# Strassen products for four pairs of gate and up rows in a fused decoder trunk, with other placement of TensorE's operands

## The chip, the cores and the metric

The kernel runs as one program on one core of a Trainium2 chip. The core has TensorE (PE, matrix multiply), VectorE (DVE), ScalarE (ACT), GpSimd (POOL) and SyncE (SP); the last only issues DMAs here. ACT and POOL issue DMAs too. Each engine works through its own queue of instructions in order and waits for the others by semaphores. The metric is the device time of one execution in microseconds (us), given as the median of several runs.

## The reference

Two decoder layers over 512 tokens of width 1024, in float32. Layer 0 mixes tokens by causal pooling, layer 1 by differential attention; each is followed by a SwiGLU feed-forward block (FFN) of width 2816.

```python
def reference(x, pool_w, pool_scale, w_qkv, w_o, lam_p, subln_g, rel_table, w_gate,
              w_up, w_down, ln_mix_g, ln_mix_b, ln_ffn_g, ln_ffn_b):
    for i in range(DEPTH):                      # DEPTH = 2
        j = i // N_MIXERS
        if i % N_MIXERS == 0:
            h = _multiscale_pool(x, pool_w[j], pool_scale[j])
        else:
            lambda_init = 0.8 - 0.6 * math.exp(-0.3 * i)
            h = _diff_attention(x, w_qkv[j], w_o[j], lam_p[j], subln_g[j], rel_table, lambda_init)
        x = _layernorm(ALPHA * x + h, ln_mix_g[i], ln_mix_b[i])
        x = _layernorm(ALPHA * x + _swiglu(x, w_gate[i], w_up[i], w_down[i]), ln_ffn_g[i], ln_ffn_b[i])
    return x

def _swiglu(x, w_gate, w_up, w_down):
    return (jax.nn.silu(x @ w_gate) * (x @ w_up)) @ w_down
```

## The kernel before

**Precision.** TensorE multiplies in a reduced float32 format (F32R). Each operand is therefore kept as two tiles: a high part, which ACT makes by a cast (line 89), and a low part, the difference, which DVE makes by a subtraction (line 90). A product is three matmuls: high by high, high by low, low by high (`mm3`, lines 106 to 110). `split` makes both parts of a tile.

**Order.** The kernel is written under a manual schedule: on each engine, and on each DMA queue, instructions run in the order in which the Python code emits them. Buffers rotate within a tag; a new tile waits until the old one in its place is no longer used.

**Weights.** All weights lie in one array `wall` in DRAM, in pieces ("chunks") of 128 by 1024. SP loads a chunk into one of 4 buffers `raw`; `split` makes the pair `wh`, `wl`, of which there are 6 buffers each (`WBUFS`). `ready(n)` emits loads and splits up to chunk n. A gate or up product of 128 hidden columns uses one chunk.

**The FFN, gate and up.** The hidden width is 22 rows of 128 columns (`FB`), kept transposed in `hid` (128 partitions, 22 rows, 512 tokens). Row f of the loop is `order[f]`: rows come in pairs k and k + 11. For each row `product` makes gate and up, each 8 blocks of 128 input channels by three matmuls, 512 tokens wide; the input is `xt`, the layer's normed and transposed input in two halves of 256 tokens with high and low parts. `gated` takes silu on ACT and the multiplication on DVE. The first `early` rows (3 in layer 0, 2 in layer 1) are done in two passes of 256 tokens, since the last two blocks of tokens are still being normed and transposed (`late`).

**The FFN, down.** The product of `hid` and the down weights is done with seven block products instead of eight (a Strassen scheme over halves of the hidden rows, tokens and output columns), named P1, Q5, P6, Q3, P7, P2, Q4 (`DOWN`). It needs sums of blocks of `hid` and sums of blocks of weights:

- `sum_weights` (line 474), 11 times per layer during gate and up: SP loads four 256 KB blocks into tiles b0 to b3, DVE adds four times (line 484), POOL writes four results to DRAM, `tsum` (line 486).
- `sum_hidden` (line 491), after each pair of rows: ACT and DVE split the first block into `a11` (lines 497, 499), DVE makes the differences in place (498, 500) and the two sums `u` (501, 504), ACT casts them to `v` (505). `settle` one product later makes the low part (508) and POOL writes both to DRAM, `ssum` (509).
- In the down stage `prepare` splits weight items a few items ahead, and `left` prepares the left operand of an item in a part of `xt` (P1 uses `a11` as it is; P7 and Q3 are loaded from `ssum` by POOL, line 566). `multiply` does 12 matmuls, 512 wide, for an item of two hidden rows (line 629).

**Other parts that the change touches.** `affine` applies a norm's gain and bias to the residual `res`, two DVE instructions of 1024 (lines 189, 190); the gain and bias come by `load_gb` into a tile of tag `gb`. Attention keeps its transposed heads in tiles `oh`, `ol` (lines 892 to 897), queries and keys in `qh`, `ql`, `kh`, `kl`; `gather` multiplies the heads with the output weights (products `wo`). `turn` transposes a block of `res` on TensorE (line 198). Tiles lie in SBUF in the order of allocation: `res` first (16 KB per partition), then small ones, `xt` (32 KB), `raw` (4 x 4 KB), `wh` and `wl` (12 x 4 KB), the rest of `keep`, and above it the pool of the current stage; in an FFN `hid` (44 KB), then `a11` (22 KB), `u`, `v` and b0 to b3.

## Time and profile before

| | |
|---|---|
| median of 3 runs | 982.99 us (979.09 to 983.11) |
| the profiled execution | 983.17 us, span of its instructions 981.1 us |
| mean granted TensorE clock | 0.995 |
| matmuls | 4974 |

In the profile's pages "PE" is TensorE's matmuls and "PEld" its weight loads, which overlap them. A row of a group names line, engine, operation, output and input tiles, shapes and count; after the first bar stand the busy time and the mean duration of one in ns, after the second the idle time of the engine before these instructions and what ended it. A matmul's duration overlaps with that of its neighbours. DMA rows give the size of one transfer and the median time from issue to landing. A row of stretches gives, for each engine, busy time and number of instructions, then TensorE's clock, the share of DMA engines' time and GB/s.

### The profile page before, as it was taken

To read this page: it belongs to the slowest core of one execution; us is meant where nothing else is said; L and a number is where in the kernel's file an instruction comes from. 1 tells how busy PE (TensorE), PEld (TensorE's weight loads), DVE (VectorE), ACT (ScalarE), POOL (GpSimd) and SP (SyncE) were. 2 spreads that over 40 slices of the span, in tenths; PEclk is the share of its full clock that TensorE was granted. 3 is DMA by queue.
4 is the path that set the end of the run, shared out by engine and by line. 5 is a ranking of instruction groups with operands and counts; after the bars stand their busy time and mean duration, and the time that the engine had idled before them with its cause. 6 is when DMAs were issued, how large, how long until landed. Compare 5 with 4: busy or idle time off the path is not lost.

```text
span 981.1 us, 13416 instructions
## 1 busy us (share of the span) xinstructions
PE 963.2 (98%) x4974; PEld 820.6 (84%) x4974; DVE 643.4 (66%) x1007; ACT 420.5 (43%) x708; POOL 123.7 (13%) x195
## 2 busy tenths in 40 slices
PE   8999999999999999999999999999999999999995
PEld 8898888888888888988888888988888888888884
DVE  6845874455567577688777676756655555477687
ACT  5753222223326357656556554732223322244460
POOL 4201111111120211000000000011111111111102
PEclk9999999999999999999999999999999999999997
DMA  8247768655776984323222122276665566878942
GB/s 223 66 158 247 250 228 289 229 193 193 266 257 236 329 295 151 114 82 94 73 87 86 55 86 86 90 270 211 225 256 193 209 229 228 288 246 297 341 145 86
DMA packets 70079, 188.59 MB, mean 192 GB/s; under 512 B 15956, under 2 KB 16084, under 8 KB 70014
## 3 DMA queue, kind: packets, MB, share of 16 engines
q1 hardware_dynamic: 56588, 141.57, 42.1%
q0 software_dynamic: 13408, 46.15, 13.9%
q8 instruction: 39, 0.64, 0.3%
q14 instruction: 26, 0.21, 0.1%
q10 hardware_dynamic: 18, 0.02, 0.0%
HBM read 150.99 MB, written 36.72 MB: 191 GB/s over the span
## 4 chain that ended last, share of the span: by engine, by line
PE 94%; DVE 3%; ACT 1%; POOL 1%; issue 0%; POOLq 0%; DVEq 0%
PE P L629 13%; PE g L109 8%; PE u L108 8%; PE u L109 8%; PE g L108 8%; PE u L110 8%; PE g L110 8%; PE Q L629 6%; PE s L814 2%; PE v L108 2%; PE v L110 2%; PE v L109 2%; PE wo L108 2%; PE wo L109 2%; PE wo L110 2%; PE q L109 1%
## 5 line engine op out<-in xcount | busy, mean ns | idle before, releaser
L90 DVE TENSOR_TENSOR wl<-raw,wh 128x1024 fp32r<-128x1024 f32 x118 | 141.7, 1220 | 33.3 <-ACT wh L89 33.3
L89 ACT CAST wh<-raw 128x1024 fp32r<-128x1024 f32 x120 | 123.5, 1050 | 65.9 <-PE u L109 63.9
L109 PE MATMUL g<-xt,wh 128*128 128x512 f32 (+1 forms) x392 | 144.1, 368 | 0.5 <-DVE xt L90 0.5
L108 PE MATMUL g<-xt,wh 128*128 128x512 f32 (+1 forms) x392 | 144.3, 368 | 0.0
L108 PE MATMUL u<-xt,wh 128*128 128x512 f32 (+1 forms) x392 | 144.1, 368 | 0.0
L110 PE MATMUL u<-xt,wl 128*128 128x512 f32 (+1 forms) x392 | 144.0, 367 | 0.0
L109 PE MATMUL u<-xt,wh 128*128 128x512 f32 (+1 forms) x392 | 144.0, 367 | 0.0
L110 PE MATMUL g<-xt,wl 128*128 128x512 f32 (+1 forms) x392 | 144.0, 367 | 0.0
L460 DVE TENSOR_TENSOR hid<-sg,u 128x512 f32<-128x512 f32 x44 | 30.3, 688 | 154.9 <-PE u L110 154.5
L90 DVE TENSOR_TENSOR dl<-r,dh 128x1024 fp32r<-128x1024 f32 x84 | 94.3, 1132 | 38.8 <-ACT dh L89 38.7
L89 ACT CAST dh<-r 128x1024 fp32r<-128x1024 f32 x84 | 81.5, 979 | 69.6 <-PE P L629 31.7
L629 PE MATMUL P<-dh,xt 128*128 128x512 f32 x352 | 109.4, 390 | 0.0
L109 PEld LDWEIGHTS g<-xt,wh 128*128 128x128 f32 x392 | 73.9, 189 | 12.7 <-DVE xt L90 0.7
L110 PEld LDWEIGHTS u<-xt,wl 128*128 128x128 f32 x392 | 73.9, 189 | 12.3
L108 PEld LDWEIGHTS u<-xt,wh 128*128 128x128 f32 x392 | 73.9, 189 | 12.1
L110 PEld LDWEIGHTS g<-xt,wl 128*128 128x128 f32 x392 | 73.9, 188 | 12.2
L108 PEld LDWEIGHTS g<-xt,wh 128*128 128x128 f32 x392 | 73.9, 188 | 12.2
L109 PEld LDWEIGHTS u<-xt,wh 128*128 128x128 f32 x392 | 73.9, 188 | 12.0
L505 ACT CAST v<-u 128x512 fp32r<-128x512 f32 x22 | 13.7, 621 | 159.4 <-issue 142.5
L629 PEld LDWEIGHTS P<-dh,xt 128*128 128x128 f32 x352 | 66.1, 188 | 13.6
L484 DVE TENSOR_TENSOR b<-b,b 128x512 f32<-128x512 f32 x88 | 60.8, 691 | 18.4 <-DMA b<-in_wall 16.2
L459 ACT ACTIVATE sg<-g 128x512 f32<-128x512 f32 x44 | 26.3, 599 | 103.5 <-PE g L110 102.0
(189 smaller groups left out, 1792.5 us busy)
## 6 DMA issues: line engine op xcount, KB each, us to landing
raw<-in_wall SPq DMA_DIRECT2D x128, 512.0 KB, 4.2
b<-in_wall SPq DMA_DIRECT2D x88, 256.0 KB, 5.6
tsum<-b POOLq DMA_DIRECT2D x88, 256.0 KB, 4.7
r<-tsum SPq DMA_DIRECT2D x40, 512.0 KB, 4.7
r<-in_wall SPq DMA_DIRECT2D x30, 512.0 KB, 5.0
ssum<-v POOLq DMA_DIRECT2D x22, 512.0 KB, 4.0
xt<-ssum POOLq DMA_DIRECT2D x20, 512.0 KB, 6.0
res<-in_x SPq DMA_DIRECT2D x8, 256.0 KB, 6.4
```

The costliest lines, as they stand in the source:

```text
L89: nc.scalar.copy(dst_h, src)
L90: (low or nc.vector).tensor_tensor(dst_l, src, dst_h.bitcast(F32), op=ALU.subtract)
L108: nc.tensor.matmul(acc, ah, bh, start=start, stop=False)
L109: nc.tensor.matmul(acc, ah, bl, start=False, stop=False)
L110: nc.tensor.matmul(acc, al, bh, start=False, stop=stop)
L459: nc.scalar.activation(sg, pg, AF.Silu)
L460: nc.vector.tensor_tensor(hid[:, f, :], sg, pu, op=ALU.mult)
L484: nc.vector.tensor_tensor(z, x, y, op=ALU.add)
L505: nc.scalar.copy(v[:, :, 0, :], u)
L629: nc.tensor.matmul(accs[s], x[:, k, r], y[:, c], start=first and k == 0 and e == 0, stop=last and k == m - 1 and e == 2, skip_group_check= ...
L814: nc.tensor.matmul(accs[c][:, :wide], a[r, qs], b[r, :wide], start=i == 0, stop=i == 2)
```

## The change

It has four parts.

1. **Strassen for gate and up.** For the pairs of rows k = 4, 6, 7 and 9 (`SPLIT`), in both layers, gate and up are computed together by the same seven-product scheme, over halves of tokens, halves of input channels, and gate against up. Each of the seven products (`GATE`) is 2 rows by 4 blocks by 3 matmuls, 256 tokens wide. Gate and up share three PSUM banks A, C and B; results are copied or subtracted out of a bank between products. The left operands are the quarters of `xt` for P1, P2 and Q4, and four sums of quarters for the others, made once per layer by `sums_of_x` in a new tile `xs`. Their right operands are sums of weight chunks, made in place in the `raw` tiles: `steps` is the written-out order of sums, casts and low parts, and `advance` emits it up to a chunk. The host lays out these chunks differently.
2. **Down sums of weights.** `load_terms` has POOL load the four blocks and then add two more loads on top of two of them (`accum_op`); `sum_terms` leaves two additions to DVE. The blocks lie in rows of `hid` that are not yet used, or in the `gb` tile, and are loaded two sums before they are used, at the rows of a list. `affine` and `load_gb` move for it (the next one behind the loop over rows, or into attention).
3. **Gated sums.** `sum_hidden` becomes a generator that `catch_up` advances one step after each product; `ssum` is written by ACT's queue. `a11` goes; P1's left operand is split in the down stage, and P6's difference is made there.
4. **Placement.** `xt`, a tile of 32 KB called `region` and the 12 weight tiles are allocated first. `region` holds in turn the pooled input, `xs` (also the down product's left operands) and attention's heads, queries and keys.

```diff
 HALF = FB // 2
 DOWN = ("P1", "Q5", "P6", "Q3", "P7", "P2", "Q4")
+SPLIT = (4, 6, 7, 9)
+GATE = ("P1", "Q5", "P6", "Q3", "P7", "P2", "Q4")
...
+    xt = keep.tile([P, 2, 2, KB, 256], F32R, name="xt")
+    def region(name):
+        return keep.tile([P, 8192], F32R, tag="region", name=name)
+    pooled = region("pooled").rearrange("p (i k t) -> p i k t", i=2, k=KB)
+    ph, pl = pooled[:, 0], pooled[:, 1]
+    def weight_pair(name):
+        return tuple(
+            keep.tile([P, 1024], F32R, tag=f"w{q}", name=f"{name}{q}", bufs=WBUFS) for q in "hl"
+        )
+    first_pair = weight_pair("pw0")
...
+            for k in range(HALF):
+                j0 = index[k] = len(chunks)
+                c = c0 + 4 * k
+                if k in SPLIT:
+                    chunks += [(c, ()), (c, (c, c + 1)), (c, (c, c + 2)), (c + 2, ())]
+                    chunks += [(c + 1, (c + 1, c + 2)), (c + 3, ()), (c, (c, c + 3))]
+                    step("cast", j0)
+                    for w in (
+                        "low 0, sum 1, cast 1, sum 4, cast 3, cast 4, low 1, sum 2, cast 2, low 3, "
+                        "low 2, sum 6, cast 5, cast 6, low 4, low 5, low 6"
+                    ).split(", "):
+                        steps.append((w[:-2], j0 + int(w[-1])))
+                else:
+                    for i in range(4):
+                        chunks.append((c + i, ()))
+                        step("cast", j0 + i)
+                        step("low", j0 + i)
...
+            def advance(upto, strict=False):
+                upto = min(upto, len(chunks))
+                while not all(j in finished for j in range(upto)):
+                    kind, j = steps.pop(1 if strict and steps[0][1] >= upto else 0)
+                    c, pair = chunks[j]
+                    refill()
+                    t = raws[c]
+                    if kind == "sum":
+                        tt(t, raws[pair[0]], raws[pair[1]], op=ALU.add)
+                    elif kind == "cast":
+                        halves[j] = weight_pair(f"g{layer}_{j}")
+                        nc.scalar.copy(halves[j][0], t)
+                    else:
+                        h, l = halves[j]
+                        tt(l, t, h.bitcast(F32), op=ALU.subtract)
+                        finished.add(j)
+                    for d in set((c,) + pair):
+                        if uses[d] == (kind, j):
+                            raws.pop(d)
+                            held[0] -= 1
...
+            def ahead(upto):
+                advance(upto)
+                if upto > len(chunks):
+                    prepare(upto - len(chunks), upto - len(chunks))
...
+            def sums_of_x():
+                r0, r1, r2, r3 = spare(4), spare(15), spare(6), spare(17)
+                def whole(t, a, b):
+                    tt(t, quarter(a, 0, b).bitcast(F32), quarter(a, 1, b).bitcast(F32), op=ALU.add)
+                def high(m, t):
+                    nc.scalar.copy(xs[:, m, 0], t)
+                def low(m, t):
+                    tt(xs[:, m, 1], t, xs[:, m, 0].bitcast(F32), op=ALU.subtract)
...
+                whole(r2, 0, 0)
+                yield
+                whole(r3, 0, 1)
+                yield
+                whole(r0, 1, 0)
+                whole(r1, 1, 1)
+                yield
+                tt(r1, r0, r1, op=ALU.subtract)
+                high(0, r1)
+                tt(r0, r2, r0, op=ALU.subtract)
+                high(2, r0)
+                yield
+                tt(r2, r1, r2, op=ALU.subtract)
+                high(1, r2)
+                low(0, r1)
+                yield
+                tt(r3, r3, r2, op=ALU.add)
+                high(3, r3)
+                low(2, r0)
+                yield
+                low(1, r2)
+                yield
+                low(3, r3)
+                yield
...
+            def load_terms(k):
+                i, j = k // 2, k % 2
+                c = slice(j * 512, (j + 1) * 512)
+                if k == 1:
+                    t = [hid[:, row, :] for row in (4, 5, 15, 16)]
+                elif k % 2 == 0 and k < HALF - 1:
+                    t = [hid[:, row, :] for row in (9, 10, 20, 21)]
+                else:
+                    rest = keep.tile([P, 4, 512], F32, tag="gb", name=f"b{layer}_{k}")
+                    t = [rest[:, q, :] for q in range(4)]
+                for q, b in enumerate((0, 1, 3, 2)):
+                    nc.gpsimd.dma_start(out=t[q], in_=block(i, b)[:, c])
+                for q, b in ((0, 1), (1, 3)):
+                    nc.gpsimd.dma_start(out=t[q], in_=block(i, b)[:, c], accum_op=ALU.add)
+                terms[k] = t
...
+            def sum_terms(k):
+                i, j = k // 2, k % 2
+                c = slice(j * 512, (j + 1) * 512)
+                t1, t3, b22, b21 = terms.pop(k)
+                tt(b22, t1, b22, op=ALU.add)
+                tt(b21, b22, b21, op=ALU.add)
+                for m, z in enumerate((t1, b22, t3, b21)):
+                    nc.gpsimd.dma_start(out=tsum[m, i, :, c], in_=z)
+            summed_rows = [0]
+            def weight_sums():
+                k = summed_rows[0]
+                summed_rows[0] += 1
+                sum_terms(k)
+                if k + 2 < HALF - 1 and k != 1:
+                    load_terms(k + 2)
+                if k == HALF - 2:
+                    load_terms(HALF - 1)
...
+            def sum_hidden(k):
+                first, second = hid[:, k, :256], hid[:, k, 256:]
+                a12, a22 = hid[:, k + HALF, :256], hid[:, k + HALF, 256:]
+                u = fp.tile([P, 2, 256], F32, tag="u", name=f"u{layer}_{k}", bufs=1)
+                v = fp.tile([P, 2, 2, 256], F32R, tag="v", name=f"v{layer}_{k}", bufs=1)
+                tt(u[:, 0, :], first, second, op=ALU.subtract)
+                tt(second, second, a22, op=ALU.subtract)
+                tt(u[:, 1, :], a12, first, op=ALU.subtract)
+                tt(u[:, 1, :], u[:, 1, :], second, op=ALU.add)
+                nc.scalar.copy(v[:, :, 0, :], u)
+                yield
+                tt(v[:, :, 1, :], u, v[:, :, 0, :].bitcast(F32), op=ALU.subtract)
+                yield
+                nc.scalar.dma_start(out=ssum[:, :, :, k, :], in_=v.bitcast(F32))
+            def catch_up():
+                for g in list(behind):
+                    if next(g, g) is g:
+                        behind.remove(g)
...
-                if p == "P1":
-                    made[j] += (a11[:, 0, r, :], a11[:, 1, r, :])
-                    return
...
+                o = 2 * (j % 2)
+                t = xs[:, j // 2 % 4, :, o : o + m, :]
...
+                    if p == "P6":
+                        tt(src, hid[:, r, 256:], src, op=ALU.subtract)
...
+            load_terms(0)
+            load_terms(1)
+            sums = sums_of_x()
...
+                        advance(2 * f + 6)
+                        gated(order[f], *accs[f])
+                        affine(n - 1, f)
+                        if f < 2:
+                            weight_sums()
+                            next(sums)
+            behind.append(sum_hidden(0))
...
+            def plain(f):
+                k = f // 2
+                j = index[k] + 2 * (f % 2)
                 a = (bank(f"g{layer}_{f}"), bank(f"u{layer}_{f}"))
                 for i in range(2):
-                    product(a[i], c0 + 2 * f + i, 0, S)
-                    if c0 + 2 * f + 5 + i <= c1:
-                        ready(c0 + 2 * f + 5 + i)
+                    product(a[i], j + i, 0, S)
+                    ahead(j + i + 5)
+                    if f >= 3:
+                        next(sums, None)
+                    catch_up()
+                gated(order[f], *a)
+                if f < SB:
+                    affine(n - 1, f)
+                if f in (3, 5, 6, 7, 10, 11, 16, 17, 20):
+                    weight_sums()
+                if f == 3:
+                    load_terms(3)
+                if f % 2:
+                    behind.append(sum_hidden(k))
+            def strassen(k):
+                names = {"P1": "A", "P6": "A", "P7": "A", "Q4": "A", "Q5": "C", "Q3": "C", "P2": "B"}
+                banks = {b: bank(f"{b}{layer}_{k}") for b in "ACB"}
+                lefts = {
+                    "P1": [quarter(0, i, 0) for i in range(2)],
+                    "P2": [quarter(0, i, 1) for i in range(2)],
+                    "Q4": [quarter(1, i, 1) for i in range(2)],
+                }
+                for m, p in enumerate(("Q5", "P6", "P7", "Q3")):
+                    lefts[p] = [xs[:, m, i] for i in range(2)]
+                rows = hid[:, k : k + HALF + 1 : HALF, :]
+                first, second = rows[:, :, :256], rows[:, :, 256:]
...
+                for j, p in enumerate(GATE):
+                    acc = banks[names[p]]
+                    h, l = halves[index[k] + j]
+                    xh, xl = lefts[p]
+                    for f in range(2):
+                        o = acc[:, f * 256 : (f + 1) * 256]
+                        for kk in range(4):
+                            c = slice((4 * f + kk) * P, (4 * f + kk + 1) * P)
+                            for e, (w, x) in enumerate(((h, xh), (h, xl), (l, xh))):
+                                nc.tensor.matmul(
+                                    o, w[:, c], x[:, kk, :],
+                                    start=p in ("P1", "Q5", "P2") and f + kk + e == 0,
+                                    stop=p in ("Q4", "Q3", "P2") and (f, kk, e) == (1, 3, 2),
+                                    skip_group_check=True,
+                                )
+                    acc = both(acc)
+                    if p == "P1":
+                        g0 = tile_of(0)
+                        nc.scalar.copy(both(g0), acc)
+                    elif p == "Q5":
+                        nc.scalar.copy(second, acc)
+                    elif p == "P6":
+                        nc.scalar.copy(first, acc)
+                    elif p == "Q3":
+                        tt(first, acc, first, op=ALU.subtract)
+                    elif p == "P7":
+                        tt(second, second, acc, op=ALU.subtract)
+                    elif p == "P2":
+                        tt(both(g0), acc, both(g0), op=ALU.add)
+                        nc.scalar.activation(g0, g0, AF.Silu)
                     else:
-                        prepare(2 * f + 5 + i - 2 * FB, 0)
-                    if i == 0:
-                        settle()
-                        if f % 2 == 0 or f in (early, FB - 1):
-                            sum_weights(summed_rows[0])
-                            summed_rows[0] += 1
-                gated(order[f], *a)
-                if f % 2:
-                    sum_hidden(f // 2)
-                if 0 < f - early <= SB:
-                    affine(n - 1, f - early - 1)
-                if f - early == SB + 2:
-                    load_gb(n)
-
-            settle()
+                        g1 = tile_of(1)
+                        nc.scalar.activation(both(g1), acc, AF.Silu)
+                    ahead(index[k] + j + 6)
+                    catch_up()
+                    if p == "P2":
+                        tt(first, both(g0), first, op=ALU.mult)
+                    elif p == "Q4":
+                        tt(second, both(g1), second, op=ALU.mult)
+                behind.append(sum_hidden(k))
...
+            whole = region("heads").rearrange("p (h i t) -> p h i t", h=HEADS, i=2)
+            slots = {h: whole[:, h] for h in range(HEADS)}
+            rest = xt[:, 1].rearrange("p i k t -> p (i k t)").rearrange("p (h i t) -> p h i t", h=4, i=2)
+            slots.update({16 + h: rest[:, h - 6] for h in (6, 7)})
...
+                oh, ol = (slots[h if h < 6 else 16 + h][:, i, :] for i in range(2))
...
+                if h == SB + 1:
+                    load_gb(n)
```

In the diff `hid`'s rows given as 9, 10, 20, 21 and 4, 5, 15, 16 are places for blocks of weights before these rows are computed; `...` marks what is left out, among it the removed `sum_weights`, `a11` and `settle`, and `product` and `gated`, which stay as they were but take the weight pair from `halves`.

198 lines of the change are left out of this document (102 added, 96 removed).

## The prediction

> **What bounds the kernel now.** First the page: busy time, granted clock, and the chain that ended last.
>
> ```profile
> PE 963.2 (98%) x4974; PEld 820.6 (84%) x4974; DVE 643.4 (66%) x1007; ACT 420.5 (43%) x708; POOL 123.7 (13%) x195
> ...
> PEclk9999999999999999999999999999999999999997
> ...
> PE 94%; DVE 3%; ACT 1%; POOL 1%; issue 0%; POOLq 0%; DVEq 0%
> ```
>
> TensorE (PE) carries 94% of the chain at full clock. Busy time alone can hide pipelining, so next the stretches by stage: gate and up of layer 0, its down product, gate and up of layer 1.
>
> ```profile
> core 0: us, PE busy (x) PEld busy (x) DVE busy (x) ACT busy (x) POOL busy (x), PEclk, DMA share, GB/s
> 60.00:284.00 224.00, 224.00 (x1058) 188.42 (x1057) 125.72 (x174) 63.44 (x85) 29.25 (x52) 1.00 0.67 230
> 284.00:383.00 99.00, 99.00 (x439) 81.54 (x438) 73.98 (x94) 50.65 (x65) 13.88 (x20) 1.00 0.75 263
> ...
> 638.00:864.00 226.00, 226.00 (x1030) 188.49 (x1029) 126.36 (x175) 63.04 (x85) 29.70 (x53) 1.00 0.67 234
> ```
>
> In these stretches PE never pauses, while VectorE (DVE) works 56% of gate and up, ScalarE (ACT) 28%. So the price of a matmul is its distance from start to start, read in the timeline (first column: start). One product of 24 matmuls, 512 wide, then one of 24, 256 wide (first and last):
>
> ```profile
> 147.93 0.39 PE L108 MATMUL u<-xt,wh 128*128 128x512 f32 x1
> ...
> 153.37 0.39 PE L108 MATMUL g<-xt,wh 128*128 128x512 f32 x1
> ```
>
> ```profile
> 43.77 0.28 PE L108 MATMUL u<-xt,wh 128*128 128x256 f32 x1
> ...
> 46.53 0.28 PE L110 MATMUL u<-xt,wl 128*128 128x256 f32 x1
> ```
>
> (153.37 - 147.93)/24 = 226.7 ns and (46.53 - 43.77)/23 = 120.0 ns. Half the width costs 0.529 of a full one.
>
> **The change, part 1: fewer columns.** A plain pair of rows (k and k+11) is 4 products, 96 matmuls: 96 x 226.7 = 21.76 us. A Strassen pair is 7 products of 24 matmuls 256 wide: 168 x 120.0 = 20.16 us. Eight pairs: -12.8 us. No row shows the new operand xs. Bounds for its matmul: 113.3 ns (half of 226.7) and 126.9 ns (120.0 plus the 6.9 ns of the next paragraph), which over 1344 matmuls is -9.0 or +9.3 us. I take 120.0, because access pattern and place in SBUF equal the quoted row's.
>
> **Part 2: operands at the low end.** Down products P1 (left operand a11) and Q5 (xt) as pieces of the chain, each of 66 matmuls, then the output projection:
>
> ```profile
> 284.10 15.35 PE P L629 x66
> 299.45 14.97 PE Q L629 x66
> ```
>
> ```profile
> 572.00 0.40 PE L108 MATMUL wo<-wh,oh 128*128 128x512 f32 x1
> ...
> 574.57 0.39 PE L110 MATMUL wo<-wh,ol 128*128 128x512 f32 x1
> ```
>
> 232.6 against 226.8 ns, and 2.57/11 = 233.6 ns. Adding up tile sizes in the code's order, xt and the weights lie in the first 113 KB, a11 begins at 169 KB, oh and ol at 179 KB; the far operands cost 6 to 7 ns more. The change brings all of these into the first 112 KB: 132 P1 matmuls x 5.8 = -0.76 us, 192 wo matmuls x 6.9 = -1.3 us. The Trainium skill (SBUF — State Buffer, § SBUF: two separate sides) lets PE wait on no one and names no dependence on the address; by it this part is worth 0 and the forecast 2 us later. The quoted rows differ, so the trace does not agree. Transposes of res, which moves up: 96 of them, at most 6.9 ns each, 0 to +0.7 us, taken as 0.
>
> Sum of PE time: -12.8 - 0.8 - 1.3 = -14.9 us.
>
> **Part 3: what the other engines get.** Groups of DVE and ACT (mean ns of one stands after the busy time), and two wide subtractions in a row:
>
> ```profile
> L90 DVE TENSOR_TENSOR wl<-raw,wh 128x1024 fp32r<-128x1024 f32 x118 | 141.7, 1220 | 33.3 <-ACT wh L89 33.3
> L484 DVE TENSOR_TENSOR b<-b,b 128x512 f32<-128x512 f32 x88 | 60.8, 691 | 18.4 <-DMA b<-in_wall 16.2
> L498 DVE TENSOR_TENSOR hid<-hid 128x256 f32<-128x256 f32 x22 | 9.3, 424 | 0.7
> L89 ACT CAST wh<-raw 128x1024 fp32r<-128x1024 f32 x120 | 123.5, 1050 | 65.9 <-PE u L109 63.9 <-issue 1.3 <-ACT line L422 0.7
> L459 ACT ACTIVATE sg<-g 128x512 f32<-128x512 f32 x44 | 26.3, 599 | 103.5 <-PE g L110 102.0
> L505 ACT CAST v<-u 128x512 fp32r<-128x512 f32 x22 | 13.7, 621 | 159.4 <-issue 142.5 <-DVE u L504 16.9
> ```
>
> ```profile
> 165.13 2.35 DVE L90 TENSOR_TENSOR wl<-raw,wh 128x1024 fp32r<-128x1024 f32 x2
> ```
>
> A wide DVE instruction lasts 1.22 us but the next starts 1.13 us later. A Strassen pair gives DVE 7 low parts and 4 sums (11 x 1.13), 5 steps on PSUM or gating (5 x 0.69) and the gated sums (4 x 0.42 + 0.69): 18.3 us of 20.16. A plain pair had 4 low parts. ACT has 7 casts, 3 copies, 2 silus, 1 cast: 11 us. Both fit; six weight buffers give five products (14 us) of lead. But a copy or subtraction out of the shared bank must end within one product (2.88 us), and that has no such lead.
>
> The tight place is the entry to a run of Strassen pairs (k = 4, 6, 9), where the row before ends with a weight sum. From the end of that row DVE does: wait for silu 0.7, gating 0.69, weight sum 1.4, sum and two low parts 3.4, gated sums 1.7: 7.9 us. Only then can ACT do the cast of v (0.62), and queued behind that cast is the copy of Q5 (0.60), which Q3 needs at 3 x 2.88 = 8.64 us. Done at 9.1: stall 0.45 us. Four such entries (k = 6, 9 in two layers): 1.8 us; k = 7, by the same count nearly level, 0.2 each.
>
> k = 4 depends on the weight sums too. DMA rows (KB, us from issue to landing) and the POOL issue:
>
> ```profile
> b<-in_wall SPq DMA_DIRECT2D x88, 256.0 KB, 5.6
> tsum<-b POOLq DMA_DIRECT2D x88, 256.0 KB, 4.7
> ...
> r<-tsum SPq DMA_DIRECT2D x8, 256.0 KB, 3.8
> ```
>
> ```profile
> L486 POOL DMA_DIRECT2D tsum<-b x88 | 48.3, 555 | 37.2 <-DVE b L484 35.5 <-DVE wl L90 1.4 <-issue 0.2
> ```
>
> A row of terms is now written out (4.7), its place reloaded (5.6), then two loads add on top. The trace has no adding load; bounds are 3.8 (the quickest load of that size) and 10.3 us (5.6 + 4.7, a read and a write in a row); I take POOL's 4.7, same queue and size. The rows wait for each other in POOL's queue: 15.0 us from one sum to terms ready. After row f = 3 two sets are loaded in series, the second only behind the first's adding loads: 21.7 us. That is needed two rows later, 21.8 us on, so any lag counts.
>
> There is lag in layer 0. Let 0 be the end of early row 0. Until the sum at f = 3 DVE has 20 wide (6 low parts, 8 affine, 6 sums of x), 11 of 512 and 4 of 256: 22.6 + 7.6 + 1.7 + 0.7 = 32.5 us, PE 2 x 5.8 + 10.9 = 22.5. Terms for f = 5 land at 32.5 + 21.7 = 54.2; DVE arrives at 47.6 and waits. That wait is covered (weights are five products ahead). But terms for f = 7 then land at 54.2 + 1.4 + 15.0 = 70.6, row f = 7 ends at 22.5 + 4 x 10.9 = 66.1, and DVE arrives near 68.5. From 70.6: 1.4 + 3.4 + 1.7 + 0.62 + 0.60 gives 78.3; Q3 wanted to start at 66.1 + 8.6 = 74.7. Stall 3.6 us. Layer 1 has one plain row more before f = 3: its f = 7 ends at 71.2, after the terms; 0.45 us.
>
> Stalls: 3.6 + 0.45 + 1.8 + 0.4 = 6.3 us.
>
> **At nothing:** affine, the gain and bias loads and the issue of ssum (POOL to ACT) only move between engines with slack in the windows above. In the down product P1's split and P6's subtraction add 0.69 each; P6 then needs 1.22 + 0.69 + 0.69 = 2.6 of PE's 2.72 us an item (12 x 226.7 ns), with four items of lead; without lead it would be level, under 1 us a layer. Weight loads leave SP, whose raw loads can only come sooner.
>
> **Sum.** The profiled execution took 983.17 us (span 981.1 and 2.1 around it), 0.2 over the median of 982.99. 983.2 - 14.9 + 6.3 = 974.6, at the median's level 974.
>
> **Rivals.** (a) *No stalls*: the load median of 5.6 us belongs to bursts behind 512 KB raw loads; if every DMA of the ring lands 1 us sooner, f = 7's terms come about 7 us sooner and PE sees nothing of them. 983.2 - 14.9 = 968. Against it: the 0.45 us entries need no DMA.
>
> (b) *The adding loads take the place of the wait, on the other side.* At 10.3 us, 5.6 more than taken, the delay enters twice before k = 4: layer 0 loses 3.6 + 11.2, layer 1 (2.0 us of slack) 9.6, others 2.2: 26.6 us, 995. It decides from the point where stalls reach 14.9 us: 6.3 + 4x - 2.0 = 14.9, x = 2.7, an adding load of 7.4 us. For it: nothing in the trace bounds such a load from above. Against: 4.7 and 5.6 us for plain ones at a DMA share of 0.67.
>
> (c) *DVE becomes the engine that bounds the pairs.* With 1.22 us a wide instruction and three waits for ACT's casts (3 x 1.05) a pair takes 19.3 + 3.2 = 22.5 us, not 20.16: 18.7 us over eight, 987. Against it: 1.13 us from start to start, and casts ordered to run beside another sum.
>
> (d) *The half-width matmul is dearer*, so that the change does not do what it says: from 21.76/168 = 129.5 ns (0.571 of a full one) the pairs gain nothing and 983.2 - 2.1 + 6.3 = 987 is left; at part 1's 126.9 ns it is 974.6 + 9.3 = 984. The row says 120.0 for the same pattern. The Trainium skill (TensorE: Matmul & The Clock Gate, § Back-to-back issue gap) gives sustained pairs of weight load and matmul about 81 ns at 128 columns and 131 at 512; an estimate between them, 98 at 256, would be 0.75 of a full one, 28.6 us a Strassen pair and some 1042 us in all. By that rule the change loses; the trace, with 226.7 and 120.0 (0.529), does not agree, so hardly any of this rival's chance is its own.
>
> **How the numbers follow.** Forecast (stalls of 3 to 10 us) 0.50; (a) 0.20; (b) 0.15, from 979 to 995; (c) 0.08; (d) 0.07. The range runs from 967, a little under (a), to 986, with about 0.13 left above and little below. About 0.5% (4.9 us) is what a measurement of this kernel can tell from no change: faster means under 978.1. Forecast and (a) give 0.70, early (b) 0.02: 0.72. Within 0.5% (978.1 to 987.9): part of (b) 0.05, most of (c) 0.06, (d) 0.07: 0.18. Slower: 0.10.
>
> **What would show it.** Strassen matmuls 120 ns from start to start, pairs of 20.2 us; P1 and wo at 227 ns; idle PE before Q3 of k = 4, mainly in layer 0, put down to ACT's copy; DVE waiting for terms at f = 5 and f = 7; an adding load landing near 4.7 us. The prediction is wrong if PE idles elsewhere, if the Strassen matmul is over 125 ns, or if the adding load lands after 7 us.

## The result, and the profile after

The changed kernel takes 987.53 us (median; 986.33 to 989.47), the kernel before beside it 982.01. The ratio (of the means) is 1.0064 with a 95% interval of 1.0044 to 1.0083: slower by 0.4 to 0.8%, where 974 was forecast. The profiled execution took 989.47 us, with a span of 987.4.

The page of the changed kernel: busy time by engine, the granted clock in 40 slices, and the chain by engine.

```profile
PE 958.6 (97%) x5550; PEld 845.4 (86%) x5550; DVE 724.7 (73%) x1069; ACT 462.8 (47%) x754; POOL 195.4 (20%) x305
...
PEclk9999988999999999999999999999999999999998
...
PE 73%; DMA 10%; DVE 7%; issue 4%; POOL 2%; ACT 2%; POOLq 0%; DVEq 0%; ACTq 0%
```

TensorE carried 94% of the chain before; now transfers, VectorE and issue gaps have 21% of it. The clock line has two eights, in slices 6 and 7 (123 to 173 us), which were nines. The stretches by stage (layer 0: up to the pair k = 4, that pair, the rest of gate and up; then the same for layer 1) say where:

```profile
core 0: us, PE busy (x) PEld busy (x) DVE busy (x) ACT busy (x) POOL busy (x), PEclk, DMA share, GB/s
60.00:131.00 71.00, 71.00 (x383) 61.74 (x382) 48.21 (x55) 19.32 (x23) 21.15 (x34) 1.00 0.76 229
131.00:161.00 30.00, 22.14 (x126) 20.91 (x125) 23.77 (x30) 12.76 (x17) 13.27 (x23) 0.77 0.89 279
161.00:290.00 129.00, 129.00 (x828) 117.85 (x827) 92.23 (x115) 52.11 (x67) 26.46 (x44) 1.00 0.72 231
638.00:724.00 86.00, 86.00 (x463) 74.75 (x463) 64.44 (x74) 31.93 (x41) 31.08 (x51) 1.00 0.81 249
724.00:737.00 13.00, 9.28 (x65) 9.07 (x64) 9.85 (x14) 5.26 (x8) 5.62 (x10) 0.87 0.98 346
737.00:864.00 127.00, 127.00 (x828) 116.55 (x827) 91.64 (x115) 51.85 (x67) 26.99 (x45) 1.00 0.73 234
```

In these stretches TensorE never pauses outside the pair k = 4, in either layer, and k = 6, 7 and 9 show no gap at all. Inside it, TensorE idles 7.9 and 3.7 us and runs at 0.77 and 0.87 of its clock. The timeline gives the length of that pair, from its first matmul to the first one of the plain pair behind it, in layer 0 and then in layer 1:

```profile
131.59 0.40 PE L798 MATMUL A<-xt,g_16h 128*128 128x256 f32 x2
...
166.62 0.40 PE L125 MATMUL g<-xt,g_23h 128*128 128x512 f32 x1
...
719.19 0.40 PE L798 MATMUL A<-xt,g_16h 128*128 128x256 f32 x2
...
744.82 0.40 PE L125 MATMUL g<-xt,g_23h 128*128 128x512 f32 x1
```

35.0 and 25.6 us, where 168 matmuls at 120.0 ns are 20.16: 14.9 and 5.5 us lost, together 20.3. Without them the span would be 967.1, which is 14.0 below the 981.1 of before: nearly all of the 14.9 us of TensorE time that were forecast did come, and 20.3 were lost in one place of each layer. The waits of TensorE in layer 0 name what it waited for (sum, count, longest):

```profile
PE C L798 <- ACT hid L809: 4.0, 1, 4.0
PE A L798 <- ACT sg L807: 2.0, 1, 2.0
PE C L798 <- ACT g_17h L555: 1.0, 1, 1.0
```

The longest is Q3 waiting for ScalarE's copy of Q5 (line 809), the second is P6 waiting for the copy of P1 (line 807), the third is Q5 waiting for its weights. Layer 1 has only the first, of 3.7 us. And these are VectorE's waits ahead of k = 4, from 60 to 131 us:

```profile
DVE hid L584 <- PE u L127: 8.6, 1, 8.6
DVE hid L597 <- DMA tsum<-hid: 5.9, 2, 5.7
DVE b L654 <- DMA b<-in_wall: 5.7, 1, 5.7
```

The first is the wait for TensorE's first result, which is due. The second is new: at f = 3 the sum of quarters of x (line 597) goes into rows 4, 5, 15 and 16 of `hid`, and these still held set 1 of the terms (what `load_terms(1)` brought), whose writes to `tsum` stood in POOL's queue behind the adding loads of set 2. The third is the wait for terms at f = 5. ScalarE's queue in layer 0 shows what such lateness does:

```profile
141.58 1.04 ACT L555 CAST g_18h<-raw 128x1024 fp32r<-128x1024 f32 x1 [3.27 <-DVE raw L552]
141.60 0.52 ACTq L686 DMA_DIRECT2D ssum<-v  x1
...
143.02 0.58 ACT L807 COPY sg<-A 128x512 f32<-128x512 f32 x1
```

The cast of a late sum of weights holds the copy of P1 (line 807), for which P6 waits. What follows is read in the chain of waits:

```profile
141.60 9.47 DMA ssum<-v
...
151.15 0.06 ACT v L682
151.68 0.59 ACT hid L809
...
152.31 5.49 PE C L798 x24
```

The write of `ssum` for k = 2 took 9.47 us to land; only then was the single tile `v` free for the cast of k = 3 (line 682), and behind that cast stood the copy of Q5. The cast also needs VectorE's u, and that was ready only at 150.8 us in VectorE's timeline, 0.3 us before the write landed.

### The profile page after: what moved, and what is told of

Same layout as the page of the kernel before. It is cut to its first block, busy times and chain, and to the rows that moved or that the text cites. A ratio compares the mean times of both kernels' runs of the same rounds, so it can differ in the third digit from the quotient of the medians.

```text
span 987.4 us, 14552 instructions
## 1 busy us (share of the span) xinstructions
PE 958.6 (97%) x5550; PEld 845.4 (86%) x5550; DVE 724.7 (73%) x1069; ACT 462.8 (47%) x754; POOL 195.4 (20%) x305
## 4 chain that ended last, share of the span: by engine, by line
PE 73%; DMA 10%; DVE 7%; issue 4%; POOL 2%; ACT 2%; POOLq 0%; DVEq 0%; ACTq 0%
PE P L862 13%; PE A L798 8%; PE Q L862 6%; PE C L798 5%; DMA hid<-in_wall 3%; DMA b<-in_wall 3%; PE g L126 3%; PE u L127 3%; PE g L127 3%; PE u L125 3%; PE g L125 3%; PE u L126 3%; DMA tsum<-hid 3%; PE B L798 2%; DMA ssum<-v 2%
## 5 line engine op out<-in xcount | busy, mean ns | idle before, releaser
L657 POOL DMA_DIRECT2D tsum<-hid x48 | 29.6, 687 | 124.2 <-DVE hid L654 120.9
L107 ACT CAST xs<-hid 128x512 fp32r<-128x512 f32 (+1 forms) x60 | 34.7, 581 | 23.0 <-DVE hid L714 23.0
L108 DVE TENSOR_TENSOR xs<-hid,xs 128x512 fp32r<-128x512 f32 (+1 forms) x60 | 38.3, 640 | 7.8 <-ACT xs L107 7.8
L217 ACT ACTIVATE y<-pt,bT,gT 128x128 f32<-128x128 f32 x96 | 36.0, 455 | 16.8 <-PE pt L212 15.8
L1062 ACT ACTIVATE p<-p,mn 128x128 f32<-128x128 f32 (+3 forms) x64 | 35.4, 553 | 14.9 <-DVE mn L1057 14.9
L552 DVE TENSOR_TENSOR raw<-raw,raw 128x1024 f32<-128x1024 f32 x32 | 39.0, 1220 | 0.6 <-DMA raw<-in_wall 0.3
L657 POOL DMA_DIRECT2D tsum<-b x40 | 23.0, 663 | 60.4 <-DVE b L654 38.7
L645 POOL DMA_DIRECT2D hid<-in_wall x48 | 27.3, 610 | 25.7 <-DMA tsum<-hid 25.3
L645 POOL DMA_DIRECT2D b<-in_wall x40 | 22.4, 631 | 49.4 <-DMA tsum<-b 49.3
L647 POOL DMA_DIRECT2D hid<-in_wall x24 | 21.1, 896 | 44.7 <-DMA hid<-in_wall 44.4
L1057 DVE CUSTOM_DVE_ANT_0 p<-s,bias 128x128 f32<-128x128 f32 (+3 forms) x64 | 28.0, 484 | 0.0
L647 POOL DMA_DIRECT2D b<-in_wall x20 | 17.5, 898 | 29.9 <-DMA b<-in_wall 29.8
L583 ACT ACTIVATE sg<-g 128x512 f32<-128x512 f32 x28 | 16.6, 592 | 13.3 <-PE g L127 13.3
```

Source lines behind the costliest of these rows:

```text
L108: (low or nc.vector).tensor_tensor(dst_l, src, dst_h.bitcast(F32), op=ALU.subtract)
L217: nc.scalar.activation(y[:, k, :], pt[:, k * P : (k + 1) * P], AF.Identity, bias=bT[:, n, kk : kk + 1], scale=gT[:, n, kk : kk + 1],)
L552: tt(t, raws[pair[0]], raws[pair[1]], op=ALU.add)
L645: nc.gpsimd.dma_start(out=t[q], in_=block(i, b)[:, c])
L647: nc.gpsimd.dma_start(out=t[q], in_=block(i, b)[:, c], accum_op=ALU.add)
L657: nc.gpsimd.dma_start(out=tsum[m, i, :, c], in_=z)
```

## The experiments

Each is an edit to the changed kernel; ratios are to the kernel before on the same chip, with 95% intervals.

**Which pair.** Only k = 4 was taken out:

```diff
-SPLIT = (4, 6, 7, 9)
+SPLIT = (6, 7, 9)
```

> Pairs k = 6, 7 and 9 stay Strassen products, k = 4 is computed plainly again, in both layers; all else is as in the changed kernel. Theory (VectorE comes to k = 4 about ten us late because it waits in program order for the ring of weight terms; there TensorE waits for ScalarE's copies out of PSUM, 14.9 us in layer 0 and 5.5 us in layer 1, and runs at half clock behind the gaps): the 20.4 us go and two pairs at 1.6 us come back, 987.5 - 20.4 + 3.2 = 970.3 us; a few us of low parts that come late may stay at f = 8 of layer 0, so 969 to 975. Rival A (VectorE has too much work in all the Strassen pairs): the wait moves to k = 6 or 7 and the time stays above 982. Rival B (the entry of a Strassen pair costs, wherever it is): 987.5 minus a quarter of the stall, about 982.

976.6 us (ratio 0.9961, 0.9945 to 0.9977): 11 us better, and still 6 above the theory (1.6 above its range). The rest is seen in ScalarE's timeline ahead of the pair that is now first, k = 6 of layer 0:

```profile
184.76 0.62 ACT L682 CAST v<-u 128x512 fp32r<-128x512 f32 x1 [3.40 <-DMA ssum<-v]
185.28 0.58 ACT L809 COPY hid<-C 128x512 f32<-128x512 f32 x1
```

The cast of v waits 3.40 us for the write of the set before, the copy of Q5 stands behind it, and TensorE waited 3.3 us at that place. But VectorE's u was ready only at 184.1 us, so without the write the cast could have come 0.6 us sooner, no more: what holds the copy up is its place behind a cast that has two late inputs. Rival A's price (over 982) did not come.

**No pair at all.** `SPLIT = ()`, the sums of x made and not read.

> No pair of gate and up is a Strassen product (the four sums of x are still made, and not read). What is left of the change: operands at the low end of SBUF, the weight sums through accumulating DMAs, the gated sums one product behind. Theory: eight pairs at 1.6 us come back and the 20.4 us of stalls in k = 4 go: 987.5 + 12.8 - 20.4 = 979.9 us, up to 984 if the low parts at f = 8 are late too. Rival A or B: also about 980, since both hang on Strassen pairs. Rival C (the rearranged sums cost TensorE time by themselves, whatever the products): 987 or more.

979.41 us (0.9983, 0.9967 to 1.0), as the theory said. Placement, weight sums and gated sums together cost TensorE next to nothing (1.6 us of waits for late weights in layer 0); the loss needs a Strassen pair behind them.

**The order of the loads at f = 3.**

```diff
+                if f == 3:
+                    load_terms(3)
                 if f in (3, 5, 6, 7, 10, 11, 16, 17, 20):
                     weight_sums()
-                if f == 3:
-                    load_terms(3)
```

> At f = 3 the loads of weight terms 3 are issued ahead of the sum and the loads of terms 4, in place of behind them, so they no longer queue behind the writes of set 2 and the adding loads of set 4. Theory: VectorE's waits at f = 5 (5.67 us in layer 0, 8.89 us in layer 1) go; VectorE reaches k = 4 that much earlier; layer 1 loses its 5.5 us, layer 0 keeps the lag of 5.66 us from f = 3 and loses about half of its 14.9 us: 987.5 - 5.5 - 7 = 975 us (971 to 980). Rival A (VectorE's work itself is too much): within 2 us of 987.5. Rival D (the adding loads are slow whatever stands ahead of them): the wait at f = 5 stays at about 5 us, within 3 us of 987.5.

992.17 us (1.0136, 1.0103 to 1.017): against theory and rivals, slower. POOL's longest wait from 60 to 140 us, in the profiled execution (998.77 us, the slowest of the four):

```profile
POOL b L645 <- DVE res L204: 22.0, 1, 22.0
```

Terms 3 go into the `gb` tile, which is in use until VectorE's last `affine` at f = 3. POOL stood 22.0 us at this load, the writes of set 2 came behind six loads of set 3, and the write of `ssum` issued at 109.44 us took 13.9 us to land, against 7.6 for the same write before the edit. The cast of v for k = 1 waited for it, and VectorE stood 8.5 us behind that cast. That the write was slow because the bursts met is likely, and not shown.

**The order, and other rows for terms 1.**

```diff
-                    t = [hid[:, row, :] for row in (4, 5, 15, 16)]
+                    t = [hid[:, row, :] for row in (3, 14, 8, 19)]
```

> The edit of the run before (terms 3 loaded ahead of the sum at f = 3), and the terms 1 in rows 3, 14, 8 and 19 of the gated products in place of 4, 5, 15 and 16, which the sums of x use too. Theory: VectorE's wait of 5.66 us at f = 3 of layer 0 goes as well as those at f = 5, no gap is left at k = 4, TensorE stays at full clock: 987.5 - 20.4 = 967 us (965 to 971), faster than before. Rival A (VectorE's work is too much): above 982. Rival E (the wait of ScalarE's cast of v for the write of ssum, 9.5 us, sets the gap): layer 0 keeps 5 to 10 us, 972 to 978.

980.58 us (1.0006, 0.999 to 1.0022), 11.6 better than with the order alone, but not the 967 of the theory. VectorE no longer waits for terms or rows ahead of k = 4; its wait of 7.9 us there is now for the cast of v for k = 1, which waited until the write for k = 0 had landed after 13.3 us. Q3 of that pair in layer 0 still waits 5.9 us for the copy of Q5. ScalarE's timeline there:

```profile
142.69 0.62 ACT L682 CAST v<-u 128x512 fp32r<-128x512 f32 x1 [3.51 <-DMA ssum<-v]
143.22 0.58 ACT L809 COPY hid<-C 128x512 f32<-128x512 f32 x1
```

The cast waits for the write, as rival E has it, but VectorE's u was ready at 142.0 us, only 0.7 us sooner, and 980.6 lies above that rival's range.

**A second place for v** (with two writes of 256 KB for these k), alone, with both edits above, and with the rows alone:

```diff
-                v = fp.tile([P, 2, 2, 256], F32R, tag="v", name=f"v{layer}_{k}", bufs=1)
+                if k in (2, 4, 6):
+                    v = hid[:, 8:20:11, :].rearrange("p m (h t) -> p m h t", h=2).bitcast(F32R)
+                else:
+                    v = fp.tile([P, 2, 2, 256], F32R, tag="v", name=f"v{layer}_{k}", bufs=1)
```

> One edit to the changed kernel: for k = 2, 4 and 6 the v of the sums of gated products lies in rows 8 and 19 of hid, which are free at that time (two writes of 256 KB in place of one of 512 KB), so that v has two places and the cast of one set no longer waits until the write of the set before has landed. The ring of weight terms is untouched. Theory (two causes in series: VectorE's lag by the ring, and the single place of v): in layer 0 VectorE writes the u of k = 3 only at 149.1 to 150.9 us, so the cast of v could start 0.2 us earlier at most and the 14.9 us stay; in layer 1 the cast waited 3.7 us for the write alone, and its 5.5 us go: 987.5 - 5.5 = 982 us (980 to 984). Rival E (the write of ssum is the whole cause): 967 to 972.

985.79 us (1.0052, 1.0034 to 1.0071): not told apart from the changed kernel. Layer 0 stayed, as the theory said; layer 1 kept a wait of 3.1 us, which the theory had down as gone. Its reading that the cast waits 3.7 us there for the write alone was wrong: in the changed kernel VectorE's u was ready at 730.4 us, and the write landed at 730.5.

> Three edits together: terms 3 loaded ahead of the sum at f = 3, terms 1 in rows 3, 14, 8 and 19, and v of k = 2, 4 and 6 in rows 8 and 19. Theory (two causes, both removed): of the 6.2 us gap and 2.4 us of slower clock that the run with the first two edits kept at k = 4 of layer 0, nothing is left; 967 us (965 to 971), and all eight Strassen pairs without a gap. Rival A (VectorE's work is too much) or B (the entry of a Strassen pair): 975 or more, the gap still at the first Strassen pair.

980.62 us (0.9989, 0.9968 to 1.0011), not 967. The gap moved from one cause to the other. The chain of waits, of this kernel:

```profile
128.17 2.83 DMA b<-in_wall
...
131.28 3.85 DMA b<-in_wall
...
136.71 0.70 DVE b L654
...
143.16 0.62 ACT v L685
143.78 0.49 ACT hid L816
...
144.31 5.49 PE C L805 x24
```

The cast of v now waits for no write but for VectorE, which does the weight sum of f = 7 at 136.7 us, behind its terms, and then one sum of weight chunks, two low parts and u before the cast can start. The copy comes at 143.8, where it came at 143.2. The edit leaves one wait for a write as it was: k = 0 and 1 still share a place, so the cast for k = 1 waited until the write for k = 0 had landed (13.0 us), and VectorE stood 7.6 us behind it. A second place for every k was not run.

> As the run with all three edits, but terms 3 are loaded where the changed kernel loads them, behind the sum at f = 3 and the loads of terms 4. It tells what the order of these loads is worth once the shared rows and the single place of v are gone. Theory: VectorE's wait at f = 5 stays at 5 to 9 us in both layers; in layer 0 it then comes to k = 4 about 5 us earlier than in the changed kernel, and a gap of 2 to 8 us is left there; layer 1 has none: 970 to 976. If the place of the loads doesn't matter, the same as the run with all three within 1 us.

976.6 us (0.995, 0.9933 to 0.9967): the order of the changed kernel is the better one by 4 us; the gap before Q3 is 4.6 us. The write for k = 0 took 7.2 us here, and VectorE stood 1.9 us behind it in place of 7.6.

**Longer runs in the write of `ssum`**, with order and rows (the write, and the loads of P7 and Q3 in two halves, follow the layout):

```diff
-            ssum = dram.tile([P, 2, 2, HALF, 256], F32, name=f"ssum{layer}")
+            ssum = dram.tile([P, HALF, 2, 2, 256], F32, name=f"ssum{layer}")
```

> Terms 3 first and terms 1 in other rows (no second place for v), and the sums of gated products laid out in memory with one run of 4 KB per partition and k in place of four of 1 KB; the loads of P7 and Q3 in the down products become two of 256 KB each in place of one. Theory F (the write lands late because it moves 512 pieces of 1 KB): it lands in under 6 us in place of 9.9, the gap of 6.0 us at k = 4 of layer 0 shrinks to 2 or less: 973 us (970 to 976). Theory G (it lands late because the loads of weights and raw weights share the DMA engines with it at that moment): it still takes 8 to 14 us and the time stays within 2 us of 980.6.

978.65 us (0.9975, 0.9959 to 0.999). The write lands sooner, as theory F says (126.98 to 131.88 us, 4.9 us in place of 9.9 for k = 2, and 7.4 in place of 13.3 for k = 0), though at k = 2 it also went out ahead of the writes to `tsum` and not beside them. The gap stays, at 6.8 us, for a reason that neither theory has:

```profile
126.98 0.33 ACTq L686 DMA_DIRECT2D ssum<-v  x1
...
143.30 0.62 ACT L682 CAST v<-u 128x512 fp32r<-128x512 f32 x1 [2.82 <-DVE u L681]
```

VectorE's u is late because VectorE waited 7.0 us for the terms of f = 7, until 136.9 us. In the run with the same order and rows the write released the cast of v at 142.7 us, here u does at 143.3; taking away one of the two gains nothing. What both hold up is the copy of Q5. So next the copy was taken out from behind the cast.

**The copies first.**

```diff
                     ahead(index[k] + j + 6)
-                    catch_up()
+                    if p not in ("P1", "Q5"):
+                        catch_up()
```

> One edit to the changed kernel: in a Strassen pair the sums of gated products that are behind are not taken up after P1 and Q5 but first after P6, so that ScalarE's copies of Q5 and P6 out of PSUM no longer queue behind the cast of v of the pair before. Theory (in layer 0 VectorE's lag holds the copies through the cast of v, which waits for VectorE's u; in layer 1 through the write of ssum): in layer 0 the copy of Q5 comes right behind the cast of the weights of P2 (148.0 us in place of 151.7), so 3.7 us of the gap go, the 7 us of late low parts and casts ahead of it stay; in layer 1 the copy comes at 728.2 in place of 731.1, 2.9 us and part of the 1.6 us of slow clock: 987.5 - 3.7 - 3.5 = 980 us (977 to 983). If the copies do not wait because of the cast of v: 987.

979.32 us (0.9974, 0.996 to 0.9989): 8 us better with no transfer and no sum changed. ScalarE in layer 0:

```profile
146.99 0.58 ACT L809 COPY hid<-C 128x512 f32<-128x512 f32 x1
```

The copy starts 0.95 us behind the cast of the weights of Q4, which is as close as casts follow each other in this queue; that is 4.7 us sooner than 151.68, and layer 1 has no wait left. In layer 0 TensorE still waits, the longest (3.5 us) for the copy of P1, which stands behind the cast of a late sum of weights.

**The copies first, the other rows, and the sum of f = 7 moved behind the pair.** The last edit:

```diff
-                if f in (3, 5, 6, 7, 10, 11, 16, 17, 20):
+                if f in (3, 5, 6, 10, 11, 16, 17, 20):
...
                     strassen(f // 2)
+                    if f == 8:
+                        weight_sums()
```

> Three edits: the copies first as in the run before; terms 1 in rows 3, 14, 8 and 19; and the weight sum of f = 7 moved behind the Strassen pair k = 4, so that VectorE has 1.4 us less to do, and no wait for its terms, ahead of that pair. Theory (what is left at k = 4 with the rows alone is VectorE's lag, fed through ScalarE's queue): no gap over 1 us at any Strassen pair, 967 us (965 to 971). Rival A (VectorE's work is too much in all pairs): the wait moves to a later pair, 975 or more.

969.57 us (0.9886, 0.9863 to 0.9909), 18 us better than the changed kernel and 1.1% faster than the kernel before. The two stretches that were bad:

```profile
131.00:161.00 30.00, 27.90 (x192) 25.67 (x191) 23.92 (x31) 12.60 (x17) 7.87 (x14) 1.00 0.97 314
...
724.00:737.00 13.00, 13.00 (x66) 11.03 (x65) 10.08 (x14) 4.86 (x7) 3.78 (x7) 1.00 0.71 264
```

192 matmuls in place of 126 in the same 30 us, at full clock. The longest wait left in these pairs is 1.5 us.

> As the run before, with the sums of gated products in runs of 4 KB, whose writes landed in 4.9 and 7.4 us in place of 9.9 and 13.3 at the same places. Theory: if nothing is left to gain there, the same as the run before within 1.5 us, 966 us; a gain of 2 us or more would say that the wait for the write still costs.

969.95 us (0.9891, 0.9867 to 0.9915): the same. ScalarE's waits of the cast of v for a write fall from four, of 21.5 us together, to one of 5.8, and TensorE gains nothing by it: its copies no longer stand behind that cast.

**The parts of the lag**, each from the changed kernel. Adds on VectorE in place of accumulating loads:

```diff
-                for q, b in ((0, 1), (1, 3)):
-                    nc.gpsimd.dma_start(out=t[q], in_=block(i, b)[:, c], accum_op=ALU.add)
...
+                tt(t1, t1, t3, op=ALU.add)
+                tt(t3, t3, b22, op=ALU.add)
                 tt(b22, t1, b22, op=ALU.add)
```

> One edit to the changed kernel: no accumulating loads; VectorE makes the two sums with two more additions per set (about 1.3 us more for each of the 11 sets of a layer). Theory (the ring of loads, adding loads and writes holds VectorE up in program order, whatever its single parts): the waits of 5.66 and 5.67 us ahead of k = 4 shrink by most of the 6 to 7 us that an adding load took to land, but six sets bring 7.5 us of work to an engine that is busy 96% of the time there; the lag stays within 4 us and the time is 983 us (979 to 988). Rival B2 (the adding loads are the cause by themselves): the lag goes and the time is 967 to 973.

981.76 us (1.001, 0.9996 to 1.0023): 5.8 better than the changed kernel, so the adding loads cost more than the additions that they save, and they are not the whole cause. Both waits of VectorE are gone, its work takes their place, and Q3 of k = 4 in layer 0 waits 6.6 us.

> One edit to the changed kernel: terms 1 in rows 3, 14, 8 and 19, which the sums of x do not use. Theory: VectorE's wait of 5.66 us at f = 3 of layer 0 goes, the wait at f = 5 stays; the lag at k = 4 is some 5 us less, so layer 0 loses 5 to 8 of its 14.9 us (with the slower clock behind the gap) and layer 1, whose wait at f = 5 is the longer one, about nothing: 980.5 us (978 to 983). If the shared rows do not matter: 987.

974.54 us (0.9931, 0.9912 to 0.9949): 13 us by four numbers of rows, twice what the theory gave. The wait at f = 3 is gone in both layers; the wait at f = 5 is still there, and now it is covered in layer 1:

```profile
DVE b L654 <- DMA b<-in_wall: 7.0, 1, 7.0
```

That is VectorE's wait in layer 1 (7.0 in place of 8.9 us), and it ends at 697.6 us, where in the changed kernel it ended at 709.1. TensorE's longest wait in that layer falls to 0.3 us.

> The copies first (the sums that are behind taken up after P6) and the other rows, with the weight sum of f = 7 where the changed kernel has it. Against the run that also moves this sum (969.6 us). Theory: the sum's 1.4 us and its wait for its terms (1.6 to 2.6 us) lie ahead of the low parts of k = 4 again, of which TensorE waits for 1 to 3 us: 972 us (970 to 975). If the place of that sum does not matter: 969.6 within 1 us.

973.09 us (0.99, 0.9863 to 0.9937). The interval overlaps that of the run with the later sum (0.9886, 0.9863 to 0.9909); what the place of that sum is worth stays open.

**More pairs**, with copies first, other rows, long runs and later sums: k = 8 too, then k = 5 as well (weight sums at f = 3, 5, 6 and behind every pair).

> As the run before, with k = 8 a Strassen pair too (weight sums at f = 3, 5, 6, 10 and 11 and behind the pairs k = 4, 6, 7 and 8). Theory: two more pairs at 1.6 us: 966 - 3.2 = 963 us (961 to 967). Rival A (VectorE is the bound where Strassen pairs follow one another): a wait at k = 8 or 9 in both layers, 967 or more.

967.88 us (0.9867, 0.984 to 0.9895): above the 961 to 967 of the theory. Waits for VectorE appear, as in rival A (up to 1.3 us in layer 0 and 1.1 in layer 1), but before Q4 of k = 6 and 7, not at k = 8 or 9.

> As the run with five pairs, with k = 5 a Strassen pair too, so that six pairs follow one another (weight sums at f = 3, 5 and 6 and behind each pair). Theory: two more pairs at 1.6 us: 967.9 - 3.2 = 964.7 us (963 to 967). Rival A (VectorE, busy 83% of the time in these pairs, bounds them when nothing plain stands between them): gaps of over 1 us in most pairs, 968 or more.

965.28 us (0.9841, 0.9804 to 0.9878): 1.6% faster than the kernel before, and within 0.6 us of what the theory gave; its four runs go from 962.87 to 971.13, and its interval overlaps that with five pairs, so the last pair's share is not told. The stretches (in the slowest of the four) with the last five pairs of layer 0 and all six of layer 1:

```profile
153.00:260.00 107.00, 104.75 (x866) 104.25 (x867) 98.49 (x119) 53.02 (x68) 24.64 (x42) 1.00 0.76 239
...
724.00:864.00 140.00, 137.31 (x1014) 131.20 (x1013) 117.77 (x148) 66.63 (x87) 28.11 (x47) 1.00 0.73 235
```

VectorE is at 92% in the first and TensorE idles 2.3 us of 107: in this form VectorE is near its bound. TensorE's waits for it are up to 1.7 us in layer 0 and 2.0 in layer 1; more pairs were not run.

## Why the prediction was wrong, point by point

**Part 1, the Strassen products: right.** Two products of k = 6 and 7, 24 matmuls each, then one with the new operand `xs`:

```profile
205.84 0.40 PE L798 MATMUL A<-xt,g_33h 128*128 128x256 f32 x2
...
211.60 0.40 PE L798 MATMUL C<-xs,g_35h 128*128 128x256 f32 x2
...
214.48 0.40 PE L798 MATMUL A<-xs,g_36h 128*128 128x256 f32 x2
```

5.76/48 and 2.88/24 are both 120.0 ns. Rival (d) is out, and with it the estimate of 98 ns from the Trainium skill (TensorE: Matmul & The Clock Gate, § Back-to-back issue gap) beside it.

**Part 2, the low end of SBUF: the numbers right.** P1 of layer 0 in the chain, and twelve matmuls of the output projection:

```profile
293.14 14.96 PE P L862 x66
```

```profile
609.67 0.39 PE L125 MATMUL wo<-w99h,xt 128*128 128x512 f32 x1
...
612.39 0.39 PE L125 MATMUL wo<-w96h,heads 128*128 128x512 f32 x1
```

14.96/66 = 226.7 and 2.72/12 = 226.7 ns, where 232.6 and 233.6 stood. By these rates the 2.1 us came. No run moves the place alone, so that the address makes the difference is still the prediction's reading and not shown.

**Part 3, the stalls: the place and the way right, the size wrong by 14 us.** Q3 of k = 4 waited for ScalarE's copy of Q5 behind the cast of v, as worked out, but the pair lost 14.9 and 5.5 us in place of 3.6 and 0.45. The step that failed is "That wait is covered (weights are five products ahead)". By the prediction's count set 3 was ready at 54.2 us and k = 4 began at 66.1, 11.9 us later. Measured, VectorE made that sum at 129.5 us (it waited until its terms had landed) and k = 4 began at 131.59: 2.1 us later, so 9.8 us of the lead were missing. Two terms account for them:

- The lag at f = 3: the count of instructions left out that the sums of x share rows with terms 1, a wait of 5.7 us. The run with four other rows shows it; it alone brings 13 us.
- The ring: 21.7 us from the sum at f = 3 to terms 3 was forecast. In VectorE's timeline that sum started at 103.62 us. The plain loads of set 3 took 6.1 to 8.6 us to land, where 5.6 were taken, and its adding load 7.44, where 4.7 were taken: the last terms that VectorE waited for came at 129.49, 25.9 us. This is 4.2 us more, and 5.7 + 4.2 = 9.9.

From there the queues ran as counted. VectorE came to the sum at f = 7 at 144.40 us, without the wait for terms that the prediction had there, and from that sum to the end of Q5's copy it took 7.9 us (7.7 by the count). The sum came 12.8 us behind the start of k = 4, where 4.5 were forecast. These 8.3 us and the 3.6 that were forecast make 11.9; measured, Q3 began 12.1 us late, and 2.8 more went to slow matmuls behind the wait. In layer 1 Q3 began 3.9 us late and 1.6 went to slow matmuls. There VectorE had waited 8.9 us at f = 5, and the slow part of the ring was the plain loads (the first of set 3, then its adding load):

```profile
693.82 9.71 DMA b<-in_wall
...
704.07 4.97 DMA b<-in_wall
```

Two things were not in the sum of the stalls at all. The issue of `ssum` was put at nothing (moved between "engines with slack"), but with one place for v it is the landing of the write that released the cast, in both layers. It came 0.3 and 0.1 us behind VectorE's u, so that removing it alone gained nothing that can be told. And the clock: behind the gaps it falls, which the sum of stalls never charged; that is the 2.8 and 1.6 us above.

**The entries of 0.45 us: did not show.** k = 6, 7 and 9 have none (129.00 busy of 129.00). With 1.4 us more work on VectorE for each weight sum they appear: three waits of 1.1 us before Q3 in layer 1 of that run, one each at k = 4, 6 and 9. So the count was right in kind and too long by at least 0.45 us.

**The rivals.** (b) decided "from an adding load of 7.4 us". The adding loads of the whole run took 4.0 to 10.4 us to land, with a median of 6.3 in place of 4.7; those of set 3 took 7.44 and 7.06 in layer 0, but 4.97 and 4.88 in layer 1. Its range (979 to 995) holds the result, in part by luck, for the runs do not make it the main cause: without adding loads 5.8 us come back, with other rows 13. (c) did not come with four pairs: VectorE has 92.23 of 129 us there. (a)'s 968 is close to what the span without the gaps gives (967.1, and some 2 us around it), and what the run with copies first, other rows and the later sum reached within 2 us.

## What to carry to other kernels

Count an engine's lag with its waits as well as its instructions: buffers that two in-order users share, and every queue between them, before a lead is called cover. A copy that frees a PSUM bank for TensorE should not stand behind work whose inputs can be late; moving it ahead was worth 8 us with nothing else made faster. When a gap stays after its named cause is removed, look for a second release at the same time, and move what both of them hold up.

## What the runs showed of the hardware

The clock falls behind short gaps. In the changed kernel, the product Q3 behind the gap and the next one in layer 0, then Q3 in layer 1 (stretches):

```profile
152.30:157.60 5.30, 5.29 (x25) 5.29 (x26) 1.47 (x2) 2.44 (x3) 3.31 (x6) 0.50 0.99 330
157.60:160.90 3.30, 3.30 (x26) 3.30 (x26) 1.82 (x2) 1.04 (x1) 0.63 (x2) 0.87 1.07 299
731.70:736.20 4.50, 4.49 (x25) 4.49 (x26) 1.70 (x2) 2.43 (x3) 2.63 (x5) 0.62 0.98 360
```

Half clock for some 6 us behind a wait of 4.0, and for part of 4.5 us behind one of 3.7: 24 matmuls took 5.3 and 4.5 us in place of 2.9, so these gaps cost 1.6 to 2.8 us more than themselves (with the start of the next product in layer 0). Shorter waits did it too, earlier in that pair:

```profile
138.10:141.40 3.30, 3.30 (x17) 3.30 (x16) 3.02 (x4) 0.21 (x1) 2.70 (x5) 0.50 0.85 222
144.90:148.20 3.30, 3.30 (x17) 3.12 (x15) 3.27 (x5) 1.05 (x1) 0.55 (x1) 0.50 1.01 349
```

The first stretch of half clock begins 0.9 us after two waits of 1.0 and 0.8 us in a row, the second 1.3 us after a wait of 2.0. The Trainium skill (TensorE: Matmul & The Clock Gate, § What's actually happening) gives half rate after an idle window of about 3.4 us. The trace agrees on the half and not on the length, by the waits just named, and a wait of one length does not always do it: in layer 1 of the run with runs of 4 KB a single wait of 2.2 us was followed by a clock of 0.63 over 4.4 us, while one of 2.0 us in the run with six pairs was followed by 1.00.

A write of 512 KB has no one time: that of `ssum` took 3.2 to 13.4 us to land in the changed kernel, with a median of 7.5, and the one that took 7.6 there took 13.9 with the other order of loads at f = 3.
